# SSD mixer: gate factors of three groups from one 104-row tile, applied in the output projection, and the state's decay taken a chunk ahead

## Chip, cores and metric

One core of one Trainium2 chip runs the whole kernel in one launch. The metric is device time in microseconds (us), the median of several runs. Beside the runs there is one profiled execution, from which all rows of the profile come. Engine names are those of the profile: PE is TensorE's matmul, PEld its weight load, DVE VectorE, ACT ScalarE, POOL GpSimd, SP the engine that issues most DMAs.

## What is computed

The reference is a decoder trunk on 1040 tokens (16 meta tokens and 1024 of the sequence) of width 1024: a Mamba-2 (SSD) mixer, a gated convolution FFN, then stick-breaking attention and a second FFN. The change concerns the mixer and the projection behind it. Cut to that:

```python
z, xbc, dt_raw = split(u @ w_in)                    # z: 2048 wide, xbc: x (2048), b, c
xbc = silu(causal_conv(xbc))
dt = softplus(dt_raw + dt_bias);  a_cs = cumsum(dt * a)      # per chunk and head
# per chunk: inside the chunk, and from the state that came into it
y_diag = einsum(cb, decay_in, xdt)
state_next = state * chunk_decay + chunk_state
y = y_diag + einsum(c, state, exp(a_cs)) + x * d_skip
hg = (y * silu(z)).reshape(b, L, G, 512)            # G = 4 groups
hg = hg * rsqrt(mean(hg * hg, axis=-1) + eps)
out = (hg * gate_g) @ w_out
```

The gate's normalisation needs, for each of 4 groups and each token, one factor r = rsqrt(mean of 512 squares + eps).

## The kernel before, in words

*Layout.* Features lie on the 128 partitions, tokens along the row. The inner width 2048 is 4 groups of 512, a group is 4 row tiles of 128 x 1040 (`rows[g][:4]`, called `xbc` in the profile), plus a B and a C tile. Tokens are cut in two ways: 3 token tiles of 348, 348 and 344 (`TT`) for projections and gates, 9 chunks of 116 (`CH`, the last 112) for the scan. A float32 product is made of three matmuls of split operands (hi x hi, lo x hi, hi x lo, L185 to L187), so a projection tile (8 row tiles of input) is 24 matmuls, and an output projection tile (4 row tiles) is 12.

*The mixer* (`mixer`, L683) interleaves two kinds of work by hand. The first is a stream of projection tiles: `blocks` is the list into(1), gate(0), into(2), gate(1), into(3), gate(2), gate(3). `into(g)` makes the convolved x, B and C of group g; `gate(g)` makes silu(z) for its four row tiles (L535), multiplies it into y (L542), squares (L547) and adds the squares up in a tile `z` (L551, L553). The second is the scan of the four groups, chunk by chunk: `ssd_front` transposes B and x, makes C x B (`cb`) on PE, masks it (`cbm`, DVE), scales x (`xdt`, DVE, then `xde`, POOL) and copies the transposed B (`bk`, ACT); `ssd_back` makes the chunk's state `S` (PE, L663), multiplies the old state by the chunk's decay (POOL, through `pieces`, L98), adds S (DVE, L670), makes the chunk's output `y` on PE (L675 from the chunk itself, L677 from the state) and adds it on DVE (L679). `ssd_decays` makes the two decay matrices `D` (DVE, ACT) and `E` (POOL) for the next chunk. Between front and back of a chunk, `SHARES` says how many tiles of the stream are taken.

*The order.* In this part the instructions of PE, DVE, ACT and POOL run in the order in which the code is written (`manual_schedule`); each engine works through its own queue and waits at an instruction whose operands aren't there. The SP queue (DMAs) is ordered by the scheduler. From `out_proj` on, the scheduler orders all.

*The gate's normalisation* is `gate_norm` (L559): `rstd` (L209 to L226) sums the squares over the partitions by a matmul with `ones` (`ms`, L218), which leaves the sum of each token on all 128 partitions, takes Ln and Exp on ACT (L221, L222) on 128 x 348, refines by four DVE operations of that size (L223 to L226), and multiplies each of the four row tiles by the factor and the gain in place (L564). It is one call for each token tile; for groups 0 to 2 the stream makes the calls ahead of tiles 0, 2 and 4 behind the gate's block, for group 3 ahead of tiles 1, 2 and 3. After the third call, groups 0 and 1 are written to DRAM by POOL (`spill`, L401, `y_d`), to be fetched again (L410) in the output projection.

*The output projection* (`out_proj`, L752) takes groups 0 to 2 one after the other: it fetches y, splits it into hi (`yh`, ACT, L195) and lo (`yl`, DVE, L196), and then for each of 8 output tiles and 3 token tiles makes 12 matmuls (`acc`) and adds the result to the stream `h` on DVE (L422). Group 3 goes into the next phase's matmuls.

Of the kernel before, what the change touches and what calls it, by code (L numbers as in the profile page):

```python
# [24 lines left out]
QW = 1056  # L25
# [44 lines left out]
ORD = ((0, 0), (1, 0), (0, 1), (1, 1), (0, 2), (1, 2))  # L70
XB, SQD = 9, (1, 4, 7)
SCALE = 0.125
SHARES = (3,) + 7 * (2,) + (1,), 3 * (4, 3, 3), 3 * (4, 3, 3), (3,) + 6 * (2,) + (3, 3)
PIECE = 256


# [24 lines left out]
class Trunk:  # L101
# [456 lines left out]

    def gate_norm(self, g, x, acc, j):  # L559
        s0, n = TT[j]  # L560
        r = self.rstd([acc.pop(j)], n, DI // GROUPS)
        for q in range(4):
            xq = x[q][:, s0 : s0 + n]
            self.nc.vector.scalar_tensor_tensor(xq, xq, self.par("gate_norm", 4 * g + q), r, op0=ALU.mult, op1=ALU.mult)  # L564

    def settle(self):

# [56 lines left out]
    def ssd_front(self, g, x, bt, ct, c, dk, pool):  # L624

        nc = self.nc
        h0 = GH * g
        tt = nc.vector.tensor_tensor
        t0, n = CH[c]
        cc = 3 * (c % 3) + c // 3  # L630
        e = t0 + n
        pcb = self.sm("cb")
        if c < 8:
            nc.tensor.transpose(pcb[:n, P : 2 * P], bt[:, t0:e], self.ident)
        nc.tensor.matmul(pcb[:n, :n], bt[:, t0:e], ct[:, t0:e], start=True, stop=True)
        px = self.lg("px")
        for q in range(4):
            nc.tensor.transpose(px[:n, q * P : q * P + P], x[q][:, t0:e], self.ident)
        px = px[:n].rearrange("p (h d) -> p h d", h=GH)
        cbm = pool.tile([P, CB], F32, tag="cbm", name=self.nm("cbm"), bufs=2)  # L640
        tt(cbm[:n, :n], pcb[:n, :n], self.past[:n, :n], op=ALU.mult)
        xdt = pool.tile([P, GH, 64], F32, tag="xdt", name=self.nm("xdt"), bufs=2)
        tt(xdt[:n], px, self.cols[:n, 0, cc, h0 : h0 + GH].unsqueeze(2).to_broadcast([n, GH, 64]), op=ALU.mult)
        tt(dk, dk, cbm[:n, :n].unsqueeze(1).to_broadcast([n, GH, n]), op=ALU.mult)
        bk = xde = None
        if c < 8:
            bk = pool.tile([P, P], F32, tag="bk", name=self.nm("bk"), bufs=2)
            nc.scalar.activation(bk[:n], pcb[:n, P : 2 * P], AF.Copy)
# [4 lines left out]
    def ssd_back(self, g, x, c, dk, ce, xdt, xde, bk, state, pool):  # L653

        nc = self.nc
        h0 = GH * g
        t0, n = CH[c]
        cc = 3 * (c % 3) + c // 3
        e = t0 + n
        new = None  # L660
        if c < 8:
            ps = self.lg("S")
            nc.tensor.matmul(ps, bk[:n], xde[:n].rearrange("p h d -> p (h d)"), start=True, stop=True)  # L663
            new = pool.tile([P, GH, 64], F32, tag="state", name=self.nm("state"), bufs=2)
            psv = ps.rearrange("p (h d) -> p h d", h=GH)
            if c == 0:
                nc.scalar.activation(new, psv, AF.Copy)
            else:
                pieces(nc.gpsimd, new, state, self.cd[:, cc, h0 : h0 + GH].unsqueeze(2).to_broadcast([P, GH, 64]), ALU.mult)
                nc.vector.tensor_tensor(new, new, psv, op=ALU.add)  # L670
        py = self.sm("y")
        for i in range(GH):
# [5 lines left out]
        for q in range(4):  # L678
            nc.vector.scalar_tensor_tensor(x[q][:, t0:e], x[q][:, t0:e], self.par("d_skip", 4 * g + q),  # L679
                                           py[:, q * CB : q * CB + n], op0=ALU.mult, op1=ALU.add)  # L680
        return new

    def mixer(self, mx):  # L683

# [4 lines left out]
        with self.tc.tile_pool(name="ssd", bufs=3) as pool:  # L689
            yd, rows = [None] * 4, [[] for _ in range(4)]  # L690
            accs = [{} for _ in range(4)]
            done, waiting = [], []

            def later(j, f):
                if 3 * j + 2 < len(done):
                    f()
                else:
                    waiting.append((j, f))

            def gate(g):  # L700
                def norm(j):
                    self.gate_norm(g, rows[g], accs[g], j)
                    if j == 2 and g < 2:
                        yd[g] = self.spill(rows[g][:4], f"y{g}_d")
                return self.gate_group(u, g, rows[g], accs[g], later if g == 3 else lambda j, f: f()) + [((0, 2, 4) if g < 3 else (1, 2, 3), norm)]

            into = lambda g: self.in_group(u, g, rows[g])
            blocks = into(1) + gate(0) + into(2) + gate(1) + into(3) + gate(2) + gate(3)
# [7 lines left out]
            with self.tc.manual_schedule(engines={E.PE, E.DVE, E.Activation, E.Pool}):  # L716
                ahead = self.ssd_decays(0, rows[0][5], 0, pool)
                dk, ce = next(ahead)
                for g in range(GROUPS):
                    *x, bt, ct = rows[g]  # L720
                    share, given = SHARES[g], 0
                    state = None
                    for c in range(9):
                        if g == c == 0:
                            next(work)
# [954 lines left out]
```

## Time and profile before

| | us |
|---|---|
| runs, median of 3 | 2958.23 (2957.75 to 2958.55) |
| the profiled execution | 2959.8 |
| its span on the core | 2958.1 |
| its mean granted clock | 0.990 |
| mixer region, by the trace | about 140 to 690 |
| output projection of groups 0 to 2 | about 690 to 832 |

The page gives for each engine its busy time, its share of the span and its number of instructions. A row of the timeline is: start, duration, engine, line, operation, out<-in with shapes, and in brackets how long the engine stood idle before it and what it waited for. A row of the waits is: engine, line and tile that waited, what was waited for, us in total, times, the longest. A row of the stretches is: from and to, length, busy time of each engine (with its instructions), the granted clock as a share of full speed, DMA share and GB/s.

### The profile page before, as it was taken

How to read it: one execution, taken by the hardware profiler on the slowest of the kernel's cores; microseconds unless marked ns; L12 is line 12 of the kernel's file. 1: busy time of each engine (PE TensorE's matmuls, PEld its weight loads, DVE VectorE, ACT ScalarE, POOL GpSimd, SP SyncE). 2: the span in 40 equal slices, each digit the busy share in tenths (PEclk: the TensorE clock that was granted, in tenths of full speed). 3: DMA queues.
4: the chain of work that ended last, by engine and by line, in shares of the span. 5: the costliest groups of instructions: out<-in, count | busy, mean ns of one | idle time of the engine just before them, and what ended most of it. 6: DMA issues, size and time to landing. Idle time of an engine off the chain costs nothing. (4 is left out here: it accounts for less than half of the span.)

```text
span 2958.1 us, 58618 instructions
## 1 busy us (share of the span) xinstructions
PE 2863.3 (97%) x21863; PEld 2724.6 (92%) x21863; DVE 2123.8 (72%) x4026; ACT 1650.7 (56%) x3398; POOL 1613.2 (55%) x2434
## 2 busy tenths in 40 slices
PE   7999998999998999999989999999999999999998
PEld 5998897889998999999989999999898999999888
DVE  5685857786468676767766888888849766767766
ACT  4555454553245665565334788888836655655433
POOL 1264545563246888876763222222353988886872
PEclk9999999999999999999999999999999999999999
DMA  5242332324122222224232122222341222225321
GB/s 164 76 113 81 107 90 96 99 85 142 56 88 76 79 75 78 80 87 174 93 125 87 55 61 67 63 65 58 101 151 59 86 82 79 76 83 178 107 100 65
DMA packets 123421, 272.80 MB, mean 92 GB/s; under 512 B 13664, under 2 KB 53216, under 8 KB 123136
## 3 DMA queue, kind: packets, MB, share of 16 engines
q1 hardware_dynamic: 117760, 257.93, 26.6%
q10 hardware_dynamic: 4112, 6.56, 0.7%
q0 software_dynamic: 1264, 4.57, 0.4%
q8 instruction: 172, 2.82, 0.4%
q14 instruction: 113, 0.93, 0.1%
HBM read 200.89 MB, written 53.20 MB: 86 GB/s over the span
## 5 line engine op out<-in xcount | busy, mean ns | idle before, releaser
L98 POOL TENSOR_TENSOR wl<-w,wh 128x256 fp32r<-128x256 f32 x780 | 692.3, 918 | 446.0 <-ACT wh L178 296.8
L185 PE MATMUL pj<-uh,wh 128*128 128x348 f32 (+2 forms) x1536 | 504.0, 329 | 9.5 <-DVE xbc L315 6.9
L186 PE MATMUL pj<-ul,wh 128*128 128x348 f32 (+2 forms) x1536 | 497.1, 324 | 0.0
L187 PE MATMUL pj<-uh,wl 128*128 128x348 f32 (+2 forms) x1536 | 494.1, 322 | 0.0
L185 PE MATMUL p<-bh,fh 128*128 128x262 f32 (+1 forms) x1408 | 400.2, 285 | 2.4 <-ACT fh L934 2.2
L187 PE MATMUL p<-bh,fl 128*128 128x262 f32 (+1 forms) x1408 | 400.6, 285 | 0.5 <-POOL fl L98 0.4
L186 PE MATMUL p<-bl,fh 128*128 128x262 f32 (+1 forms) x1408 | 400.0, 285 | 0.1
L98 POOL TENSOR_TENSOR fl<-x,fh 128x256 fp32r<-128x256 f32 x352 | 260.0, 771 | 159.0 <-ACT fh L934 134.6
L186 PE MATMUL p<-bl,wh 128*128 128x262 f32 (+1 forms) x1056 | 301.1, 285 | 6.3 <-DVE bl L887 6.1
L185 PE MATMUL p<-bh,wh 128*128 128x262 f32 (+1 forms) x1056 | 301.5, 286 | 5.1 <-ACT ft L982 4.2
L185 PEld LDWEIGHTS pj<-uh,wh 128*128 128x128 f32 x1536 | 290.6, 189 | 12.9 <-issue 10.1
L187 PE MATMUL p<-bh,wl 128*128 128x262 f32 (+1 forms) x1056 | 301.0, 285 | 0.0
L186 PEld LDWEIGHTS pj<-ul,wh 128*128 128x128 f32 x1536 | 291.1, 190 | 1.4 <-issue 0.5
L315 DVE SCALAR_TENSOR_TENSOR c<-p,params,c 128x260 f32<-128x260 f32 (+1 forms) x528 | 249.5, 480 | 58.4 <-ACT c L312 51.6
L187 PEld LDWEIGHTS pj<-uh,wl 128*128 128x128 f32 x1536 | 290.5, 189 | 0.6 <-issue 0.6
L185 PEld LDWEIGHTS p<-bh,fh 128*128 128x128 f32 x1408 | 267.7, 190 | 3.4 <-ACT fh L934 2.9
L186 PEld LDWEIGHTS p<-bl,fh 128*128 128x128 f32 x1408 | 267.6, 190 | 0.6 <-DVE bl L887 0.3
L187 PEld LDWEIGHTS p<-bh,fl 128*128 128x128 f32 x1408 | 266.8, 190 | 1.4 <-POOL fl L98 1.2
L982 ACT ACTIVATE ft<-p 128x262 f32<-128x262 f32 (+1 forms) x352 | 133.2, 383 | 184.2 <-DVE p L985 109.2
L187 PE MATMUL acc<-gh,wl 128*128 128x260 f32 (+1 forms) x672 | 213.8, 320 | 2.8 <-POOL wl L98 2.8
L185 PE MATMUL acc<-gh,wh 128*128 128x260 f32 (+1 forms) x672 | 211.1, 320 | 3.1 <-DVE h L1133 3.1
L186 PE MATMUL acc<-gl,wh 128*128 128x260 f32 (+1 forms) x672 | 213.9, 319 | 0.0
(314 smaller groups left out, 7965.9 us busy)
## 6 DMA issues: line engine op xcount, KB each, us to landing
w<-in_w_up SPq DMA_DIRECT2D x88, 512.0 KB
w<-in_w_down SPq DMA_DIRECT2D x44, 512.0 KB
w<-in_w_in SPq DMA_DIRECT2D x40, 512.0 KB
E<-ea_d SPq DMA_DIRECT2D x32, 464.0 KB
D<-acs_d SPq DMA_DIRECT2D x32, 420.5 KB
g<-c SPq DMA_DIRECT2D x88, 130.0 KB
g<-c SPq DMA_DIRECT2D x88, 128.0 KB
b<-g SPq DMA_DIRECT2D x16, 520.0 KB
```

Of the source, the lines that this page charges most:

```text
L98: eng.tensor_tensor(out[:, c], x[:, c], y[:, c], op=op)
L185: mm(out, wh, uh, start=first, stop=False, skip_group_check=joins)
L186: mm(out, wh, ul, start=False, stop=False, skip_group_check=joins)
L187: mm(out, wl, uh, start=False, stop=last, skip_group_check=joins)
L315: nc.vector.scalar_tensor_tensor(out, ps[:, o + i : o + i + n], wcol(i), out, op0=ALU.mult, op1=ALU.add)
L982: nc.scalar.activation(s[:, :N], ps[:, :N], AF.Copy)
```

## The change

Four edits:

1. *Gate factors.* For groups 0 to 2 `gate_norm` only makes the sums with the `ones` matmul, copies one row of them (ACT), and sends it to DRAM (`ms_d`, 3 x 1040). One more tile of the stream after the last chunk, `gate_factors` reads all 3 x 1040 sums as a tile of 104 partitions x 30 (40 bytes in a piece), makes the three groups' factors there in one go (Ln, Exp, three DVE operations) and writes them to DRAM (`gr_d`). In `out_proj` each group fetches its row of factors, spread over 128 partitions (`r`), and multiplies its four row tiles in place (12 DVE products, L792) before the split. Group 3 is normalised as before.
2. *When.* The calls for groups 0 to 2 come ahead of tiles 1, 2 and 3 behind the gate's block instead of 0, 2 and 4; the spill of groups 0 and 1 comes ahead of the first call, before the normalisation.
3. *State.* POOL multiplies the new state by the next chunk's decay at the end of `ssd_back` (`scaled`); the next `ssd_back` only adds S to it.
4. *Small moves.* `bk` is copied ahead of `cbm` in `ssd_front`; in the last chunks of group 3 one tile of the stream moves from between front and back of chunk 7 to behind the scan (SHARES).

The diff, without comment lines and the arguments that only follow:

```diff
-SHARES = (3,) + 7 * (2,) + (1,), 3 * (4, 3, 3), 3 * (4, 3, 3), (3,) + 6 * (2,) + (3, 3)
+SHARES = (3,) + 7 * (2,) + (1,), 3 * (4, 3, 3), 3 * (4, 3, 3), (3,) + 7 * (2,) + (3,)
...
     def gate_norm(self, g, x, acc, j):
         s0, n = TT[j]
+        if g < 3:
+            ps, sums = self.sm("ms"), acc.pop(j)
+            self.nc.tensor.matmul(ps[:, :n], self.ones, sums[:, :n], start=True, stop=True)
+            self.nc.scalar.activation(sums[:1, :n], ps[:1, :n], AF.Copy)
+            self.nc.sync.dma_start(self.ms_d[g : g + 1, s0 : s0 + n], sums[:1, :n])
+            return
...
+    def gate_factors(self):
+        nc = self.nc
+        m, k, width = 104, 10, DI // GROUPS
+        s, y, b = (self.tmp("gf")[:m, : 3 * k] for _ in range(3))
+        view = lambda d: d.rearrange("g (p c) -> p g c", c=k)
+        nc.sync.dma_start(s.rearrange("p (g c) -> p g c", c=k), view(self.ms_d))
+        self.ln_exp()
+        nc.scalar.activation(y, s, AF.Ln, scale=1.0 / width)
+        nc.scalar.activation(y, y, AF.Exp, scale=-0.5)
+        nc.vector.tensor_tensor(b, y, y, op=ALU.mult)
+        nc.vector.scalar_tensor_tensor(b, b, -0.5 / width, s, op0=ALU.mult, op1=ALU.mult)
+        nc.vector.scalar_tensor_tensor(y, b, 1.5, y, op0=ALU.add, op1=ALU.mult)
+        nc.sync.dma_start(view(self.gr_d), y.rearrange("p (g c) -> p g c", c=k))
...
+        bk = xde = None
+        if c < 8:
+            bk = pool.tile([P, P], F32, tag="bk", name=self.nm("bk"), bufs=2)
+            nc.scalar.activation(bk[:n], pcb[:n, P : 2 * P], AF.Copy)
         cbm = pool.tile([P, CB], F32, tag="cbm", name=self.nm("cbm"), bufs=2)
...
-        bk = xde = None
         if c < 8:
-            bk = pool.tile([P, P], F32, tag="bk", name=self.nm("bk"), bufs=2)
-            nc.scalar.activation(bk[:n], pcb[:n, P : 2 * P], AF.Copy)
...
             else:
-                pieces(nc.gpsimd, new, state, self.cd[:, cc, h0 : h0 + GH].unsqueeze(2).to_broadcast([P, GH, 64]), ALU.mult)
                 nc.vector.tensor_tensor(new, new, psv, op=ALU.add)
...
-        return new
+        scaled = None
+        if c < 7:
+            scaled = pool.tile([P, GH, 64], F32, tag="state", name=self.nm("state"), bufs=2)
+            cn = 3 * ((c + 1) % 3) + (c + 1) // 3
+            pieces(nc.gpsimd, scaled, new, self.cd[:, cn, h0 : h0 + GH].unsqueeze(2).to_broadcast([P, GH, 64]), ALU.mult)
+        return new, scaled
...
                 def norm(j):
+                    if j == 0 and g < 2:
+                        yd[g] = self.spill(rows[g][:4], f"y{g}_d")
                     self.gate_norm(g, rows[g], accs[g], j)
-                    if j == 2 and g < 2:
-                        yd[g] = self.spill(rows[g][:4], f"y{g}_d")
-                return self.gate_group(u, g, rows[g], accs[g], later if g == 3 else lambda j, f: f()) + [((0, 2, 4) if g < 3 else (1, 2, 3), norm)]
+                return self.gate_group(u, g, rows[g], accs[g], later if g == 3 else lambda j, f: f()) + [((1, 2, 3), norm)]
...
+                next(work)
+                self.gate_factors()
                 for _ in work:
                     pass
...
         for g in range(3):
-            ops = [self.split(ys[g][q] if yd[g] is None else self.fetch(yd[g][q], "y"), "y") for q in range(4)]
+            r = self.rp.tile([P, QW], F32, tag="r", name=self.nm("r"))
+            self.nc.sync.dma_start(r[:, :L], self.gr_d[g : g + 1].to_broadcast([P, L]))
+            y = [ys[g][q] if yd[g] is None else self.fetch(yd[g][q], "y") for q in range(4)]
+            for s0, n in TT:
+                for q in range(4):
+                    c = slice(s0, s0 + n)
+                    self.nc.vector.scalar_tensor_tensor(y[q][:, c], y[q][:, c], self.par("gate_norm", 4 * g + q), r[:, c], op0=ALU.mult, op1=ALU.mult)
+            ops = [self.split(t, "y") for t in y]
```

The number of rows per engine stays on PE and POOL, DVE has 33 fewer, ACT 15 fewer, SP 14 more.

**POOL's order**, in group 1 of the scan, where group 0's spill falls (a row is line, operation, out<-in, shape, pieces; `state`, `xde`, `E` are as above, `wl` is the low part of a projection weight). Before:

```order
L98 TENSOR_TENSOR state_3027<-state_2820,cd 128x256 x2
L98 TENSOR_TENSOR xde_3067<-xdt_3062,cols 116x256 x2
L98 TENSOR_TENSOR wl_3121<-w_386_3118,wh_3120 128x256 x4
L401 DMA y_d<-xbc_544 128x1040
L401 DMA y_d<-xbc_678 128x1040
L401 DMA y_d<-xbc_788 128x1040
L401 DMA y_d<-xbc_903 128x1040
L98 TENSOR_TENSOR E_3116<-E_3116,xbc_2158 128x232 x4
L98 TENSOR_TENSOR state_3222<-state_3027,cd 128x256 x2
L98 TENSOR_TENSOR xde_3262<-xdt_3257,cols 116x256 x2
```

Now:

```order
L98 TENSOR_TENSOR E_2900<-E_2900,xbc_2163 128x232 x4
L401 DMA y_d<-xbc_546 128x1040
L401 DMA y_d<-xbc_680 128x1040
L401 DMA y_d<-xbc_790 128x1040
L401 DMA y_d<-xbc_905 128x1040
L98 TENSOR_TENSOR state_3049<-state_2847,cd 128x256 x2
L98 TENSOR_TENSOR xde_3067<-xdt_3064,cols 116x256 x2
L98 TENSOR_TENSOR wl_3111<-w_385_3108,wh_3110 128x256 x4
L98 TENSOR_TENSOR E_3106<-E_3106,xbc_2163 128x232 x4
L98 TENSOR_TENSOR state_3219<-state_3049,cd 128x256 x2
```

The four spill DMAs stand a chunk earlier and no longer behind the products of L564; the state row, which had stood between its own chunk's `E` and the next `xde`, now makes the state for the chunk that follows.

**DVE's order** at the normalisation of a token tile of group 2. Before:

```order
L644 TENSOR_TENSOR D_6065<-D_6065,cbm_6147 116x928
L553 TENSOR_TENSOR z_5562<-z_5562,z_6094 128x348
L542 TENSOR_TENSOR xbc_3470<-xbc_3470,z_6182 128x344
L223 TENSOR_TENSOR z_5529<-y_6203 128x348
L224 TENSOR_TENSOR z_5529<-z_5529,ms_6201 128x348
L225 TENSOR_SCALAR z_5529<-z_5529 128x348
L226 TENSOR_TENSOR y_6203<-y_6203,z_5529 128x348
L564 TENSOR_SCALAR xbc_2959<-xbc_2959,params,y_6203 128x348
L564 TENSOR_SCALAR xbc_3127<-xbc_3127,params,y_6203 128x348
L564 TENSOR_SCALAR xbc_3308<-xbc_3308,params,y_6203 128x348
L564 TENSOR_SCALAR xbc_3470<-xbc_3470,params,y_6203 128x348
L553 TENSOR_TENSOR z_5600<-z_5600,z_6182 128x344
```

Now the eight rows L223 to L564 are gone there, and twelve products with the factors (L792) stand at the junction to the output projection, ahead of the twelve lo parts. The last four of these and what stands behind them:

```order
L196 TENSOR_TENSOR yl_6813<-y_6792,yh_6812 128x344
L196 TENSOR_TENSOR yl_6821<-y_6794,yh_6820 128x344
L196 TENSOR_TENSOR yl_6829<-y_6796,yh_6828 128x344
L196 TENSOR_TENSOR yl_6837<-y_6798,yh_6836 128x344
L553 TENSOR_TENSOR z_6299<-z_6299,z_6732 128x344
L223 TENSOR_TENSOR z_6170<-y_6742 128x348
L422 TENSOR_TENSOR h_6851<-h_6851,acc_6854 128x348
L422 TENSOR_TENSOR h_6955<-h_6955,acc_6958 128x348
L422 TENSOR_TENSOR h_6851<-h_6851,acc_6868 128x348
L224 TENSOR_TENSOR z_6170<-z_6170,ms_6740 128x348
```

Group 3's own normalisation, which stays, now follows group 0's products and lo parts, and all of these stand ahead of the first add L422.

**SP's order** at the junction, now:

```order
L410 DMA y_6796<-y_d 128x1040
L410 DMA y_6798<-y_d 128x1040
L172 DMA w_838_6948<-in_w_out_f 128x512
L172 DMA w_845_7000<-in_w_out_f 128x512
L578 DMA gf_6636<-ms_d 104x3x10
L172 DMA w_852_7052<-in_w_out_f 128x512
L585 DMA gr_d<-gf_6637 104x3x10
L787 DMA r_6790<-gr_d 128x1040
L172 DMA w_859_7104<-in_w_out_f 128x512
L410 DMA h_6851<-h_d 128x1040
L410 DMA h_6903<-h_d 128x1040
```

The read of the sums, the write of the factors and the broadcast read stand in one queue, with the fetches of `h` behind them; before, those followed the fetches of y and the weights at once.

More of the change, by code (lines that the diff above doesn't have):

```diff
@@ L651, in ssd_front, with ssd_back @@
         return xdt, xde, bk
-    def ssd_back(self, g, x, c, dk, ce, xdt, xde, bk, state, pool):
+    def ssd_back(self, g, x, c, dk, ce, xdt, xde, bk, states, pool):
         nc = self.nc
@@ L659, in ssd_back @@
         e = t0 + n
-        new = None
+        state, new = states
         if c < 8:
@@ L663, in ssd_back @@
             nc.tensor.matmul(ps, bk[:n], xde[:n].rearrange("p h d -> p (h d)"), start=True, stop=True)
-            new = pool.tile([P, GH, 64], F32, tag="state", name=self.nm("state"), bufs=2)
             psv = ps.rearrange("p (h d) -> p h d", h=GH)
             if c == 0:
+                new = pool.tile([P, GH, 64], F32, tag="state", name=self.nm("state"), bufs=2)
                 nc.scalar.activation(new, psv, AF.Copy)
             else:
-                pieces(nc.gpsimd, new, state, self.cd[:, cc, h0 : h0 + GH].unsqueeze(2).to_broadcast([P, GH, 64]), ALU.mult)
                 nc.vector.tensor_tensor(new, new, psv, op=ALU.add)
@@ L692, in mixer @@
             done, waiting = [], []
+            self.ms_d, self.gr_d = (self.dp.tile([3, L], F32, tag=t, name=t) for t in ("ms_d", "gr_d"))
             def later(j, f):
@@ L721, in mixer @@
                     share, given = SHARES[g], 0
-                    state = None
+                    state = None, None
                     for c in range(9):
```

## Prediction

> **What bounds the kernel now.** I read the head of the page first, then the busy time stretch by stretch, then TensorE's (PE's) waits, and last the timeline around the longest of them.
>
> The head of the page, span and PE's row:
>
> ```profile
> span 2958.1 us, 58618 instructions
> PE 2863.3 (97%) x21863; PEld 2724.6 (92%) x21863; DVE 2123.8 (72%) x4026; ACT 1650.7 (56%) x3398; POOL 1613.2 (55%) x2434
> ```
>
> PE is the bound over the whole span: 2958.1 - 2863.3 = 94.8 us are all that it stands idle. The change adds no matmul and takes none away (the three `ones` products of a group stay), so it can gain only idle time of PE and time in which PE runs below its full clock. Both are to be looked for in the mixer, the only part it touches besides the first groups of the output projection.
>
> Busy time by stretch; the columns are the stretch and its length, then PE, PEld, DVE, ACT and POOL busy with their instructions, the granted clock, DMA share and GB/s:
>
> ```profile
> 281.00:349.00 68.00, 58.21 (x378) 53.40 (x377) 50.07 (x107) 31.97 (x45) 32.68 (x45) 0.90 0.32 105
> 349.00:440.00 91.00, 91.00 (x680) 86.08 (x680) 60.19 (x135) 46.45 (x69) 43.60 (x57) 1.00 0.28 82
> 440.00:503.00 63.00, 52.29 (x356) 47.84 (x355) 45.31 (x94) 30.07 (x44) 32.66 (x45) 0.95 0.31 101
> 503.00:545.00 42.00, 42.00 (x301) 39.96 (x301) 35.96 (x72) 21.50 (x31) 22.88 (x33) 1.00 0.35 103
> 545.00:640.00 95.00, 86.67 (x661) 78.84 (x660) 74.42 (x150) 50.34 (x73) 55.31 (x70) 0.99 0.31 99
> 640.00:690.00 50.00, 49.74 (x353) 46.31 (x354) 35.66 (x80) 29.17 (x48) 23.52 (x30) 0.95 0.20 64
> ```
>
> The first, third and fifth stretch hold the gate normalisations of groups 0, 1 and 2. There PE is idle 9.8, 10.7 and 8.3 us, and its clock falls. The second and fourth run the same chunks and the same tiles without a gate normalisation: PE 100% busy at clock 1.00. So the normalisations, not the scan as such, make the gaps. The size of it, by matmul count: the two undisturbed stretches pass 981 matmuls in 133 us, 135.6 ns each; the other four hold 1748, which at that pace take 237 us and took 276. **39 us** are recoverable if all were as smooth. The second way to count: idle 9.8 + 10.7 + 8.3 + 0.3 = 29.1 us, and clock 68 x 0.10 + 63 x 0.05 + 95 x 0.01 + 50 x 0.05 = 13.4 us, together 42.5.
>
> What PE waits for in the mixer (us in total, times, longest):
>
> ```profile
> PE ms L218 <- DVE z L553: 9.6, 2, 4.9
> PE S L663 <- POOL xde L98: 8.9, 6, 4.3
> PE pj L185 <- DVE xbc L315: 6.9, 2, 3.9
> PE S L663 <- ACT xbc L312: 2.1, 1, 2.1
> PE cb L635 <- ACT xbc L503: 1.6, 1, 1.6
> PE y L675 <- DVE D L644: 1.3, 1, 1.3
> ```
>
> The first four rows make 27.5 us. The timeline at the first `ms` gap shows what stands behind it:
>
> ```profile
> 282.91 1.18 POOL L98 TENSOR_TENSOR state<-state,cd 128x256 f32<-128x256 f32 x2
> 284.13 0.69 DVE L670 TENSOR_TENSOR state<-state,S 128x512 f32<-128x512 f32 x1 [3.01 <-POOL state L98]
> 285.72 0.27 DVE L641 TENSOR_TENSOR cbm<-cb,past 116x116 f32<-116x116 f32 x1
> 286.02 0.28 ACT L648 ACTIVATE bk<-cb 116x128 f32<-116x128 f32 x1 [6.96 <-DVE cbm L641]
> 287.54 0.93 DVE L553 TENSOR_TENSOR z<-z,z 128x348 f32<-128x348 f32 x1
> 288.52 1.53 PE L218 MATMUL ms<-z,ones 128*128 128x348 f32 x2 [4.86 <-DVE z L553]
> ```
>
> VectorE (DVE) stands 3.0 us for POOL's multiplication of the state; so the next chunk's `cbm` is late; so ScalarE (ACT) stands 6.96 us in front of `bk`, with the gate's silu and square behind it; so the sum of squares is late, and PE stands 4.86 us at `ms`. Waits of the whole mixer that belong to this chain, and the one on the spill:
>
> ```profile
> ACT bk L648 <- DVE cbm L641: 76.8, 29, 8.5
> DVE state L670 <- POOL state L98: 18.8, 6, 3.6
> POOL y_d L401 <- DVE xbc L564: 18.4, 2, 9.2
> ```
>
> **The change, part by part.**
>
> *State times decay a chunk ahead.* The same 56 POOL pieces, but issued at the end of a chunk for the next. DVE's 18.8 us of waiting go. POOL now stands there for the chunk's `y` matmuls to free the old buffer, with `xde` and `E` of the next chunk queued behind; in the undisturbed stretches POOL is busy 43.6 of 91 us, which hides that. Without that cover it would be a later `xde`, which is in the 8.9 us above already. Worth nothing alone where PE is at 100%; in the gate stretches it is the first link of the chain.
>
> *bk ahead of cbm on ACT.* ACT no longer waits for DVE (29 times, 2.6 us on average); instead `cbm` on DVE now waits for ACT's `bk`, a copy of 0.28 us. What is queued behind `cbm` on DVE is `xdt` and the D product, which feed POOL's `xde` and PE's `y`. Since ACT was the one that stood waiting in 29 of 32 chunks, it should mostly be there first. I price the new wait at 0; the other end is in the rivals.
>
> *Normalisation out of the mixer.* Per group DVE loses twelve row operations of four kinds and twelve L564 products. The two outer ones of the four kinds, and L564:
>
> ```profile
> L564 DVE SCALAR_TENSOR_TENSOR xbc<-xbc,params,y 128x348 f32<-128x348 f32 (+1 forms) x48 | 32.0, 728 | 0.4
> L223 DVE TENSOR_TENSOR z<-y 128x348 f32<-128x348 f32 (+1 forms) x12 | 8.1, 675 | 22.9 <-ACT y L222 21.2 <-PE S L663 1.7
> L224 DVE TENSOR_TENSOR z<-z,ms 128x348 f32<-128x348 f32 (+1 forms) x12 | 6.2, 513 | 0.3
> ```
>
> That is 12 x 0.73 + 12 x 0.59 = 16 us per group off the engine at which the waits of these stretches end, and the idle time ahead of L223 with it. The POOL spill of `y_d` no longer waits for the twelve products: its 18.4 us stood in front of `E`, state and `xde`, so the 8.9 us of PE at `S` should go as well. `ms` comes one tile (3.75 us, below) later, which gives the late sum of squares that much more room than the 4.9 us it lacked; with DVE's 3 us that is more than enough.
>
> What stays are the two short waits of the scan's own, 1.6 and 1.3 us. Nine one-row ACT copies and nine small SP writes take the place of 18 Ln and Exp passes on an ACT that is about half busy, and the tile that SHARES moves behind the last chunk of group 3 is the same tile: both priced at 0. I take **-38** of the 39 to 42.5; the low bound is the gaps that go by the chain alone, 9.6 + 8.9 + 2.1 + 3.4 of the third row = **-24**, the high one **-43**.
>
> *The new piece at the junction.* This runs before the output projection and has no cover but the last three projection tiles. Prices, from these rows:
>
> ```profile
> 775.00:800.00 25.00, 25.00 (x160) 25.00 (x159) 11.26 (x20) 4.64 (x8) 5.77 (x8) 1.00 0.13 42
> 686.00:745.00 59.00, 56.84 (x347) 54.42 (x347) 38.60 (x77) 23.39 (x47) 17.03 (x26) 1.00 0.44 159
> 691.49 1.28 ACT L209 ACT_TABLE_LOAD   x1
> L490 SPq DMA_DIRECT2D acs_d<-rows x3: 341/420/422, 100.1 to 100.9; - x3
> L606 SPq DMA_DIRECT2D D<-acs_d x36: 266/270/1507, 102.9 to 628.0; - x36
> 683.22 1.11 SPq L410 DMA_DIRECT2D y<-y_d  x2
> 686.87 1.26 ACT L195 ACTIVATE yh<-y 128x348 fp32r<-128x348 f32 x3 [3.28 <-DMA y<-y_d]
> 645.23 2.06 DVE L564 SCALAR_TENSOR_TENSOR xbc<-xbc,params,y 128x348 f32<-128x348 f32 x4
> 704.71 3.02 DVE L564 SCALAR_TENSOR_TENSOR xbc<-xbc,params,y 128x348 f32<-128x348 f32 x4
> 690.81 1.37 DVE L196 TENSOR_TENSOR yl<-y,yh 128x348 fp32r<-128x348 f32 x3
> L422 DVE TENSOR_TENSOR h<-h,acc 128x348 f32<-128x348 f32 (+1 forms) x35 | 17.4, 512 | 23.6 <-PE acc L187 20.6 <-DMA h<-h_d 3.0
> ```
>
> PE passes 160 matmuls in 25 us, 156 ns each: 3.75 us for a projection tile of 24, 1.88 us for an output tile of 12. A write to DRAM and the dependent read take 2.0 us from issue to issue (100.9 to 102.9); a broadcast read about 3.65 us (683.22 to 686.87). A product on DVE takes 0.515 us when POOL is quiet (645.23, four in 2.06), 0.755 when it is not (704.71).
>
> Let T be the end of the projection tile behind which `gate_factors` stands in the order; three tiles are left, so PE would begin the output projection at T + 11.4. The chain for `r`: ACT's queue ahead (a silu, squares, one `wh`), a table load and Ln, Exp on 30 columns, T + 4; three small DVE operations, T + 5; write to DRAM, T + 7; broadcast back, T + 10.7. Then twelve products of group 0 on DVE, 6.2 to 9.1 us, T + 17 to 18; then `yl` at 0.46 each. PE can take the first `yl` at about T + 18.5 and stands **7 us**. The twelve `yl` and the squares between them end at T + 26. Behind them stand, in DVE's written order, twelve products each of groups 3, 1 and 2, twelve small operations of group 3 and 14 adds L422 that empty PE's accumulators: 36 x 0.515 + 12 x 0.59 + 14 x 0.51 = 32.7 us, and about 1.5 more where POOL is in the way (busy 17 of 59 us there): T + 60. PE may be two or three accumulators ahead of the adds, 17 tiles, 32 us, which it would have had at T + 43.4 without any wait. So **DVE, not PE, sets the time for some 50 us here**, and PE loses 17 us. At the start of group 1 its `yl` stand behind ten adds: 2 more. Before, this stretch lost time too: 347 matmuls at 0.156 are 54 us of 59, and some matmul records may be missing; I take 4. Net **+15**. The bounds: +4, if the fetch comes early and POOL stays away from DVE (the first wait of 7 less some 3), and +28, if the products all cost 0.755 (36 x 0.24 = 8.6) and the r chain is 4 us longer. Off this stretch nothing changes.
>
> **Sum.** -38 + 15 = -23 us. The profiled execution took 2959.8 us, 1.7 above its span and 1.6 above the median of the runs (2958.23). 2958.2 - 23 gives **2935 us**. A measurement of this kernel can tell about 0.2%, 6 us, from no change.
>
> **A rule beside the rows.** On the clock: in the stretch from 281 us PE is idle 9.8 of 68 us, and the mean granted clock is 0.90. The Trainium skill ("TensorE: Matmul & The Clock Gate", section "What's actually happening") says the clock is halved after an idle window of about 3.4 us and comes back after about as long a busy one; by that, only the four gaps above 3.4 us (two at `ms`, one at `S`, one at `pj`) cost clock, some 1.7 us each, an estimate of 7 us in place of the 13.4, so the second way to count would give 36. The trace agrees in direction: no clock below 1.00 where there is no gap.
>
> **Rivals.**
>
> - *The junction is nearly free* (+4): -34, **2924 us**. For it: the DVE row of the 686 us stretch shows 20 us of slack in 59. Against: the change puts 24 products more into just this place.
> - *The next wait takes over*: half of the mixer's gaps stay, since DVE remains 66 to 75% busy and PE waits for `xbc` L315 (6.9 us), which has no link to any edit. -20 + 15 = -5, **2953 us**.
> - *POOL and DVE get in each other's way at the junction*: 86 DVE rows (twelve products and twelve `yl` of group 0, then the 62) at 0.24 us more each, +20: -38 + 15 + 20 = -3, **2955 us**. For it: 3.02 against 2.06 us for the same four products. Against: POOL is busy only 17 of 59 us there. The Trainium skill ("SBUF — State Buffer", section "Who interferes with whom") states the same as a rule: a DVE instruction with two inputs in SBUF contends with a POOL instruction that reads SBUF, and the shared ports are locked for a whole instruction. The products at L792 have two such inputs; the two rows above agree.
> - *Slower: cbm now waits for ACT.* Where ACT reaches `bk` late, behind a table load of 1.28 us, every one of the 32 chunks puts that on DVE, and through `xdt` and `xde` on PE: 32 x 1.28 = 41 us. -38 + 41 + 15 = +18, **2976 us**. It decides from the point at which ACT comes to `bk` later than DVE to `cbm`; before, ACT was there first 29 times, by up to 8.5 us.
> - *It doesn't do what it says*: the state's wait returns as one for `S` or `y`, DVE is as late as before, and only the later `ms` (9.6) and some of the spill's 8.9 are gained: -15 + 15 = 0, **2958 us**.
>
> **Chances.** Forecast 0.46 (own range 2926 to 2947), free junction 0.12, next wait 0.15, contention 0.12, cbm 0.10, no effect 0.05. Faster by over 0.2% (below 2952): 0.46 + 0.12 + 0.12 from the lower parts of the third and fourth = 0.70. Within: 0.07 + 0.07 + 0.03 = 0.17. Slower: 0.13. The range 2921 to 2958 leaves out the cbm case, the ends of the others, and half of no effect: 0.2.
>
> **What would show it.** In the stretches of groups 0 to 2, PE's waits at `ms` and at `S` for `xde` gone and the clock at 1.00; no wait of DVE for state and none of ACT at `bk`. At the junction, PE waiting for `yl` about 7 us once, then for adds L422, DVE close to 100% for some 40 us, `r` landing 10 to 11 us behind the tile. It would be wrong if DVE shows a wait at `cbm` for ACT of over 0.5 us in most chunks, if L315 becomes PE's longest wait, or if products L792 cost over 0.7 us on average.

## The result, and the profile after

| | us |
|---|---|
| before, median of the runs beside it | 2958.39 |
| the changed kernel, median of 4 runs | 2932.39 (2932.11 to 2939.06) |
| ratio to before, 95% interval | 0.9909 (0.9897 to 0.9922) |
| forecast | 2935, range 2921 to 2958 |

The kernel is 26 us faster, clear of the 0.2% that can be told apart. The head of the changed kernel's page:

```profile
span 2930.6 us, 58544 instructions
PE 2852.6 (97%) x21863; PEld 2717.9 (93%) x21863; DVE 2074.8 (71%) x3993; ACT 1629.3 (56%) x3379; POOL 1620.1 (55%) x2434
```

The span is 27.5 us shorter; PE's idle time went from 94.8 to 78.0 us, and its busy time fell by 10.7 us with the same 21863 matmuls. That fits the clock: the mean granted clock went from 0.990 to 0.993, which over the two spans makes 9 us less lost to the clock. The stretches of the mixer that had the gaps, and the two between, now (columns as before the change):

```profile
281.00:349.00 68.00, 68.00 (x498) 63.75 (x497) 47.86 (x110) 34.78 (x52) 39.14 (x56) 1.00 0.39 119
349.00:440.00 91.00, 91.00 (x659) 86.53 (x658) 54.09 (x129) 44.53 (x68) 47.72 (x61) 1.00 0.29 87
440.00:503.00 63.00, 63.00 (x468) 59.22 (x467) 42.94 (x95) 31.05 (x47) 38.65 (x56) 1.00 0.43 134
503.00:545.00 42.00, 42.00 (x312) 39.29 (x310) 25.47 (x64) 21.61 (x33) 18.07 (x23) 1.00 0.31 105
545.00:640.00 95.00, 94.59 (x747) 87.39 (x747) 60.17 (x151) 50.31 (x76) 58.79 (x76) 1.00 0.32 96
```

PE is busy all the time and the clock is 1.00 in every row. In the first row 498 matmuls pass where 378 passed before. The four longest waits of PE from 140 to 690 us:

```profile
PE acc L186 <- DVE yl L196: 3.3, 1, 3.3
PE acc L185 <- DVE h L422: 2.4, 1, 2.4
PE y L696 <- DVE D L669: 1.5, 1, 1.5
PE S L685 <- POOL xde L98: 1.4, 2, 1.0
```

The waits at `ms` (9.6) and `pj` (6.9) are gone, the one at `S` for `xde` went from 8.9 to 1.4; the two longest rows are new and belong to the junction. The other engines, from 140 to 640 us:

```profile
POOL state L98 <- DVE state L691: 56.7, 15, 5.5
...
ACT bk L664 <- PE cb L656: 5.3, 5, 1.8
...
DVE cbm L666 <- ACT bk L664: 1.9, 2, 1.2
```

DVE's wait for POOL's state (18.8) has turned round: POOL waits for DVE, 56.7 us, and no engine waits for POOL's state any more (PE still waits 1.4 us for its `xde`). ACT's 76.8 us at `bk` behind `cbm` are gone: what is left are 5.3 us for PE's `cb`, and `cbm` waits for ACT twice.

**Where the time went, in two pieces.** The first matmul of the output projection, and the last one of its 24th tile, before:

```profile
686.30 0.32 PE L185 MATMUL acc<-yh,wh 128*128 128x348 f32 x1
...
735.53 0.32 PE L187 MATMUL acc<-yh,wl 128*128 128x344 f32 x1
```

and now, with the chain of the factors between (SPq is SP's queue):

```profile
635.97 1.28 ACT L209 ACT_TABLE_LOAD   x1
637.26 0.23 ACT L580 ACTIVATE gf<-gf 104x30 f32<-104x30 f32 x1
638.24 0.19 DVE L584 SCALAR_TENSOR_TENSOR gf<-gf,gf 104x30 f32<-104x30 f32 x1
638.46 0.34 SPq L585 DMA_DIRECT2D gr_d<-gf  x1
640.41 0.33 SPq L787 DMA_DIRECT2D r<-gr_d  x1
644.00 6.93 DVE L792 SCALAR_TENSOR_TENSOR y<-y,params,r 128x348 f32<-128x348 f32 x12 [0.70 <-DMA r<-gr_d]
...
645.34 0.59 PE L185 MATMUL acc<-yh,wh 128*128 128x348 f32 x1
...
650.85 0.94 DVE L196 TENSOR_TENSOR yl<-y,yh 128x348 fp32r<-128x348 f32 x2
652.58 4.37 DVE L196 TENSOR_TENSOR yl<-y,yh 128x348 fp32r<-128x348 f32 x10
...
705.62 0.32 PE L187 MATMUL acc<-yh,wl 128*128 128x344 f32 x1
```

PE reaches the output projection 686.30 - 645.34 = **41 us earlier**. Its first 24 tiles then take 705.6 - 645.3 = 60.3 us where they took 49.2: **11 us are given back**. The output tiles of groups 1 and 2, counted in the same way by the starts of their matmuls, take 0.9 and 0.2 us longer than before, and what follows them 1.4, which makes the 27.5 of the spans.

### The profile page after: what moved, and what is told of

Its sections match the earlier page's. It is cut to its first block, busy times and chain, and to the rows that moved or that the text cites. A ratio compares the mean times of both kernels' runs of the same rounds, so it can differ in the third digit from the quotient of the medians.

```text
span 2930.6 us, 58544 instructions
## 1 busy us (share of the span) xinstructions
PE 2852.6 (97%) x21863; PEld 2717.9 (93%) x21863; DVE 2074.8 (71%) x3993; ACT 1629.3 (56%) x3379; POOL 1620.1 (55%) x2434
## 4 chain that ended last, share of the span: by engine, by line
PE 44%; DVE 2%; ACT 2%; POOL 1%; issue 1%; DMA 0%; DVEq 0%; ACTq 0%; SPq 0%; POOLq 0%
PE p L187 5%; PE p L186 5%; PE p L185 5%; PE acc L185 4%; PE acc L187 4%; PE acc L186 4%; PE pj L185 3%; PE pj L187 3%; PE pj L186 3%; PE po L1444 3%; PE wT L1430 2%; PE lg L1403 2%; POOL wl L98 1%; PE ms L897 0%; DVE h L1138 0%
## 5 line engine op out<-in xcount | busy, mean ns | idle before, releaser
L315 DVE SCALAR_TENSOR_TENSOR c<-p,params,c 128x260 f32<-128x260 f32 (+1 forms) x528 | 249.2, 480 | 58.7 <-ACT c L312 51.9
```

The source lines that it names most:

```text
L315: nc.vector.scalar_tensor_tensor(out, ps[:, o + i : o + i + n], wcol(i), out, op0=ALU.mult, op1=ALU.add)
```

## The experiments

Each kernel is compared with the kernel before on the same chip; ratios carry 95% intervals. The last two columns come from the one profiled execution of each: the start of the first matmul of the output projection, and the time from there to the start of the 288th, which ends its 24th tile.

| kernel | median us | ratio to before | first output matmul | 24 tiles |
|---|---|---|---|---|
| before | 2958.39 | 1 | 686.3 | 49.2 |
| changed | 2932.39 | 0.9909 (0.9897 to 0.9922) | 645.3 | 60.3 |
| scan edits alone | 2943.08 | 0.9942 (0.9930 to 0.9955) | 665.7 | 49.3 |
| gate edits alone | 2948.36 | 0.9963 (0.9949 to 0.9977) | 661.5 | 62.2 |
| changed, state in its own chunk | 2939.18 | 0.9930 (0.9917 to 0.9942) | 648.2 | 60.4 |
| changed, bk behind cbm | 2935.89 | 0.9920 (0.9906 to 0.9933) | 645.8 | 61.5 |
| changed, spill after the calls | 2934.35 | 0.9913 (0.9898 to 0.9927) | 644.5 | 65.1 |
| changed, calls at 0, 2, 4 | 2934.75 | 0.9914 (0.9899 to 0.9929) | 644.9 | 62.1 |
| changed, old SHARES | 2937.11 | 0.9927 (0.9913 to 0.9941) | 648.5 | 61.6 |
| changed, factors early | 2922.68 | 0.9871 (0.9855 to 0.9888) | 645.0 | 52.7 |
| changed, 24 products left out | 2925.58 | 0.9883 (0.9869 to 0.9898) | 645.2 | 53.9 |
| changed, 24 products held back | 2927.82 | 0.9896 (0.9882 to 0.9909) | 645.1 | 58.5 |
| factors early, 24 products held back | 2919.71 | 0.9868 (0.9855 to 0.9882) | 645.4 | 53.1 |
| factors early, 24 products left out | 2916.56 | 0.9860 (0.9847 to 0.9874) | 644.8 | 49.1 |

Behind the output tiles of groups 0 to 2 stands code that none of these edits touches. In the fourteen profiled executions it takes 2127 to 2134 us, so a few us between two medians can come from there; the last two columns don't have that part.

### Which edits carry the mixer

**The scan's edits alone**: the kernel before with `ssd_front` and `ssd_back` of the changed one.

```diff
+            bk = pool.tile(...)                        # ahead of cbm
...
-                pieces(nc.gpsimd, new, state, self.cd[:, cc, ...], ALU.mult)
...
+            pieces(nc.gpsimd, scaled, new, self.cd[:, cn, ...], ALU.mult)
```

> The kernel before, with the two edits of the scan alone: the state multiplied a chunk ahead, and bk copied ahead of cbm. The gate normalisation, its call points and the spill stay as before. Theory (the normalisations in the mixer make the gaps, the state's wait is only their first link): the wait at ms (9.6 us of PE) goes, most of the waits behind the spill stay; about -12, 2946 us, and the clock in the three gate stretches still below 1.00. Rival (the state's wait is the cause): nearly the whole mixer gain without the price of the junction, -38, 2920 us.

Measured: -16 us (2943.08), between the two, nearer to the theory. Two stretches with a gate normalisation, and PE's longest wait:

```profile
281.00:349.00 68.00, 63.22 (x428) 59.42 (x428) 56.52 (x115) 36.00 (x51) 38.48 (x52) 0.95 0.35 107
...
440.00:503.00 63.00, 58.14 (x400) 54.53 (x399) 52.57 (x108) 34.37 (x48) 32.80 (x46) 0.95 0.33 103
```

```profile
PE pj L185 <- DVE xbc L315: 9.6, 4, 4.5
PE S L664 <- POOL xde L98: 4.5, 4, 2.7
```

The wait at `ms` is gone and the clock stays below 1.00 in the gate stretches, as the theory had it; of the 8.9 us at `S`, half went too. What stays is DVE: busy 56.5 of 68 us, it makes PE wait for the conv tile L315.

**The gate's edits alone**: the changed kernel, with the two edits of the scan undone.

```diff
-            nc.scalar.activation(bk[:n], pcb[:n, P : 2 * P], AF.Copy)     # ahead of cbm
+            nc.scalar.activation(bk[:n], pcb[:n, P : 2 * P], AF.Copy)     # behind the D product
...
-            pieces(nc.gpsimd, scaled, new, self.cd[:, cn, ...], ALU.mult)
+                pieces(nc.gpsimd, new, state, self.cd[:, cc, ...], ALU.mult)
```

> The changed kernel with the state multiplied in its own chunk and bk copied behind cbm, as before: only the gate factors, the call points and the spill are changed. Theory: 10 us above the changed kernel, 2942 us, since with 16 us of DVE work per group gone the state's wait has nothing behind it that is late. Rival (the state's wait is the cause): the mixer gains nothing and the junction costs 12 us, 2970 us.

Measured: 16 us above the changed kernel where 10 were expected. PE still waits at `ms`, and the timeline shows another chain than before:

```profile
PE ms L563 <- DVE xbc L700: 9.6, 3, 4.1
```

```profile
299.82 2.18 POOL L401 DMA_DIRECT2D y_d<-xbc  x4
302.01 1.19 POOL L98 TENSOR_TENSOR state<-state,cd 128x256 f32<-128x256 f32 x2
303.24 0.69 DVE L691 TENSOR_TENSOR state<-state,S 128x512 f32<-128x512 f32 x1 [3.78 <-POOL state L98]
303.84 1.07 DVE L700 SCALAR_TENSOR_TENSOR xbc<-xbc,params,y 128x116 f32<-128x116 f32 x4
304.82 0.27 DVE L663 TENSOR_TENSOR cbm<-cb,past 116x116 f32<-116x116 f32 x1
...
305.06 1.49 PE L563 MATMUL ms<-z,ones 128*128 128x344 f32 x2 [4.06 <-DVE xbc L700]
305.13 0.28 ACT L669 ACTIVATE bk<-cb 116x128 f32<-116x128 f32 x1 [6.87 <-DVE cbm L663]
305.30 0.43 ACT L564 ACTIVATE z<-ms 1x348 f32<-1x348 f32 x1
```

The spill's four issues (2.18 us of POOL) stand ahead of the state; DVE waits 3.78 us for it; its adds of `y` (L700) are late, and PE's `ms` waits for them although it uses nothing of `y`. By the code, `ms`, `cb` and `y` share three small accumulators. No view shows which of them a matmul got; from the wait I take it that this `ms` was given the one that L700 empties. ACT, which would empty the earlier `ms` (L564), stands 6.87 us at `bk`. So the gate's edits by themselves put a new wait in the place of the old one.

**One of the two edits of the scan undone at a time:**

> The changed kernel with the state multiplied in its own chunk again; bk stays ahead of cbm. Theory: DVE waits for POOL's state again, some 20 us in all, PE hardly; +4, 2936 us. Rival (the state's wait is the cause): +25 or more, 2957 us.

> The changed kernel with bk copied behind cbm again. Theory: ACT stands at bk for DVE again, half as long as before since DVE is less late; +3, 2935 us. Rival (ACT standing at bk is what made the square sums late): +10 or more, 2942 us. If cbm's new wait for ACT costs something, this kernel is faster than the changed one.

Measured: +6 us by the ratios (0.9930 against 0.9909) and +3, both with intervals that overlap the changed kernel's. Together the two were worth 16. The traces show it more sharply: without one of them PE reaches the output projection 2.9 us later (the state) or 0.5 (`bk`), without both 16.2 us later. So either of them covers most of the other's loss. In the kernel with the state in its own chunk, DVE still waits 19.6 us for it, but ACT doesn't stand behind it. At the same place as above:

```profile
298.42 0.26 ACT L664 ACTIVATE bk<-cb 116x128 f32<-116x128 f32 x1
298.58 0.43 ACT L564 ACTIVATE z<-ms 1x348 f32<-1x348 f32 x1
...
301.08 0.74 PE L563 MATMUL ms<-z,ones 128*128 128x344 f32 x2
...
303.49 0.69 DVE L692 TENSOR_TENSOR state<-state,S 128x512 f32<-128x512 f32 x1 [3.79 <-POOL state L98]
```

`bk` and the row copy come 6.7 us earlier, and `ms` runs before DVE has the state, so here it can't have been given the accumulator of `y`; one that ACT had emptied was free. With `bk` behind `cbm` and the state ahead, ACT waits 48.8 us at `bk`, but DVE has no wait to pass on. `cbm` waiting for ACT costs nothing: the kernel without it isn't faster.

By the first matmul of the output projection (661.5 with the gate's edits, 665.7 with the scan's, 645.3 with both) the mixer gains 25, 21 and 41 us: nearly the sum. Neither half alone is "the cause"; both make DVE less late.

**Spill and call points:**

```diff
-                    if j == 0 and g < 2:
-                        yd[g] = self.spill(rows[g][:4], f"y{g}_d")
                     self.gate_norm(g, rows[g], accs[g], j)
+                    if j == 2 and g < 2:
+                        yd[g] = self.spill(rows[g][:4], f"y{g}_d")
```

> The changed kernel with the spill of groups 0 and 1 after the third gate call again, not ahead of the first. Theory: what held the spill before was the wait for the twelve products on DVE, which are gone; nothing stands in front of it, 0, 2932 us. Rival (POOL's place for the spill itself matters): +4 or more, 2936 us.

```diff
-((1, 2, 3), norm)
+((0, 2, 4) if g < 3 else (1, 2, 3), norm)
```

> The changed kernel with the gate calls of groups 0 to 2 ahead of tiles 0, 2 and 4 again. Theory: the first ms comes a tile earlier and the square sums are no longer late by 4.9 us but still by about a tile's work of ACT and DVE: PE waits about 2 us for each of three groups, +5, 2937 us. Rival (the later call is all that removed the wait at ms): +10 with the clock down again, 2942 us. Second rival (it doesn't matter any more): 0.

Measured: 2934.35 and 2934.75, both within the interval of the changed kernel, and both with PE busy 68.00 of 68.00 us at clock 1.00 in the first stretch; PE reaches the output projection within 1 us of the changed kernel. Neither the place of the spill nor the later call, undone alone, costs the mixer anything. Both undone together was not run, so it isn't shown that neither covers for the other. The +5 expected of the calls was a miss.

### What the junction costs

**Factors early**: `gate_factors` after chunk 7 of group 3, where its sums are already in DRAM.

```diff
+                            if c == 7:
+                                self.gate_factors()
...
-                next(work)
-                self.gate_factors()
```

> The changed kernel with gate_factors called after chunk 7 of group 3 instead of one tile after chunk 8, four projection tiles earlier: the factors and the first broadcast are in place and the twelve products of group 0 done before the last projection tile ends. Theory 1 (both the chain and the amount of DVE work at the junction cost): the wait for yl goes, and twelve products, 7 us, leave the stretch in which DVE is the bound; -8, 2924 us. Theory 2 (DVE's amount of work alone sets the junction): -7 from the twelve products that move, the same. Rival (the products now stand in the mixer and delay the scan's last chunk): 0 to +5, 2933 to 2937 us.

Measured: 2922.68, about 10 us below the changed kernel; the first 24 tiles take 7.6 us less. The broadcast is issued at 623.5, the products stand at 627 and 631, and PE:

```profile
640.00:690.00 50.00, 45.45 (x278) 43.98 (x277) 40.68 (x85) 17.54 (x33) 18.11 (x23) 1.00 0.49 172
```

against the same 50 us of the changed kernel:

```profile
640.00:690.00 50.00, 40.40 (x232) 38.09 (x230) 46.70 (x93) 17.27 (x31) 19.08 (x18) 0.93 0.51 187
```

46 matmuls more and no clock lost. The mixer pays nothing: PE reaches the output projection at 644.96.

**24 products left out, or held back on DVE:**

```diff
-            for s0, n in TT:
+            for s0, n in TT if g == 0 else ():
```

> The changed kernel without the 24 products of groups 1 and 2 in the output projection, so these two groups go into it without their normalisation. Theory (DVE is the bound at the junction): 12 or 13 us of DVE work gone from it, of which the part behind the first wait shows; -7, 2925 us. Rival (only the chain of the factors costs, the adds L422 are hidden anyway): -1 or less, 2932 us.

```diff
                 for s0, n in TT:
                     self.accumulate(h, f, s0, n, ..., ops, HB)
+                    if g < 2 and 2 <= f < 6:
+                        self.tc.keep_in_program_order(product(g + 1, r, y, f - 2, s0, n))
```

> The changed kernel with the products of groups 1 and 2 held back in the same way, and the factors where the change has them. Theory: the wait for the chain of the factors stays (7 us of PE at the first output tiles), the 24 products leave the crowded stretch: like the kernel that leaves them out, -6, 2926 us. Rival: the chain alone sets the junction, 0, 2932 us.

Measured: -7 us without them, -4 or -5 with them held back (the second with an interval that overlaps the changed kernel's); in the 24 tiles -6.4 and -1.8. Chain and amount are two costs: without the 24 products the wait for `yl` stays (3.3 us in the waits, as in the changed kernel), with the early factors the wait is gone and the adds stay late.

**Both together:**

> The kernel with gate_factors after chunk 7, and besides the products of groups 1 and 2 held back on DVE: those of a group stand one after each add of output tiles 2 to 5 of the group before. Theory (what is left of the junction's cost is DVE's amount of work): 24 output tiles, which took 52.7 us with the early factors and would take 47 without a wait, come down by 4; 2919 us. Rival (the rest is something else, a weight's low part or the order of group 3's own products): 0, 2923 us. Second rival (a product between two adds delays the adds): +3, 2926 us.

> The kernel with gate_factors after chunk 7, without the 24 products of groups 1 and 2, so these two groups go into the projection without their normalisation: what holding them back can bring at most. Theory: -5 against the early factors alone, 2918 us, and PE waits for no add in the first 24 output tiles. Rival (chain and amount are one cost, counted twice): no gain over the early factors, 2923 us.

Measured: 2919.71 and 2916.56. Holding back on top of the early factors brings 1 us by the ratios (0.9868 against 0.9871) and 3 by the medians: not told apart from nothing. The 2919 us of the theory came by luck: the 24 tiles, which were to come down by 4 us, take 53.1 where they took 52.7; the twelve products of group 1 still stand among them, and why moving the other twelve brings nothing there was not traced. The tiles of group 1 take 1.6 us less, and the rest of the 3 us lies behind them. Leaving the products out brings 3 to 6 us by the runs and 3.6 in the 24 tiles, which then take 49.1, as before the change. So chain and amount together are all that the change lost there. What is left on DVE there are its other rows: group 3's own normalisation, and the adds. The 50 us from 640 in the kernel without the 24 products:

```profile
640.00:690.00 50.00, 48.55 (x301) 47.65 (x300) 30.25 (x62) 18.17 (x34) 16.39 (x25) 1.00 0.48 173
```

DVE falls to 30 of 50 us, and PE is back at 48.55. The kernel with early factors beats both the kernel before and the changed one; holding the products back as well is the fastest that computes all, by less than the measurement can tell.

**The old SHARES:**

> The changed kernel with the old SHARES of group 3: its eighth-from-last tile order is as before, so one tile of the stream stands between front and back of the last chunk but one and gate_factors comes a tile later in the order. Theory: the factors come one tile, 3.75 us, nearer to the output projection and the first wait grows by as much; +3, 2935 us. Rival: 0, 2932 us, since the wait for the amount of DVE work behind covers it.

Measured: 2937.11, about 5 us above the changed kernel by the ratios, the two intervals just overlapping. PE's waits at the junction have a row that the changed kernel has at 0.7 us:

```profile
PE acc L185 <- DVE h L422: 5.1, 2, 3.1
PE acc L185 <- ACT yh L195: 3.1, 1, 3.1
PE acc L186 <- DVE yl L196: 2.5, 1, 2.5
```

With one tile fewer behind it, the chain of the factors comes out later for PE: the first output matmul starts 3.2 us later, and the 24 tiles take 1.3 us more.

## Why the prediction was right, and where it was not

- **What is recoverable in the mixer: right, slightly small.** Forecast -38 out of 39 by matmul count and 42.5 by idle time and clock; measured 41, between the two counts. The term was undersized by 3. The rival of a next wait that takes over (2953) fell: the one at L315 went with the others.
- **Which step carries it: right in direction, the shares not worked out.** The prediction gave one sum for all edits of the mixer: the state's wait as the first link, and 16 us of DVE work per group as the weight behind it. The expectation for the gate's edits alone, 10 us above the changed kernel, held that without this work nothing late stands behind the state's wait. That was too strong: 16 us are lost, by a wait that the prediction did not see, `ms` standing until DVE's adds of `y` are done. The scan's edits alone gave 16 where 12 were expected. Inside the gate's edits, the products, the four small DVE operations and ACT's Ln and Exp went together; which of them counts most was not tested.
- **The new wait of cbm for ACT, priced at 0: right.** It is 1.9 us on DVE in two chunks; the slower rival (1.28 us in each of 32 chunks) did not come about. ACT, which used to stand waiting here, is now there first in nearly all chunks, as the prediction had it.
- **The spill and the later call:** the wait of the spill went, and `S` with it, but by the products' going, not by the new place; the later `ms` was credited with room that wasn't needed.
- **The junction: right in its mechanism; +15 was forecast, 12 measured** (11 in the first 24 tiles, 1 in the tiles of groups 1 and 2; the free junction, +4, did not come about). By its own steps, with T = 633.9, the end of the projection tile ahead of `gate_factors`: factors ready T + 4.5 (T + 5 was forecast), broadcast landed T + 10 (10.7), products done T + 17 (17 to 18), PE 7 us late (the first twelve output matmuls run from 645.34 to 654.39, 9 us where 2 are needed; 7 was forecast as standing), DVE through at T + 57 (T + 60). That the 7 came out is in part luck: PE stands 4.6 us (3.3 of them at `yl`), and part of the rest is a granted clock of 0.50 from 648.2 to 655.1, which the prediction did not count here. The row that bears out "DVE, not PE, sets the time":

```profile
644.00:691.00 47.00, 36.95 (x209) 34.65 (x208) 45.86 (x91) 16.43 (x29) 19.27 (x19) 0.93 0.51 187
```

  DVE is busy 45.9 of 47 us. The kernels with early factors and without the 24 products split it: by the runs some 10 us for the chain and group 0's products, some 7 for the other 24, 14 to 16 for both; in the 24 tiles 7.6, 6.4 and 11.2.
- **Contention, the rival at 2955: did not come about.** The products at L792 cost 0.58 each for group 0 (6.93 for twelve) and 0.50 where twelve stand together at 684 us, near the price with a quiet POOL.

```profile
L792 DVE SCALAR_TENSOR_TENSOR y<-y,params,r x24: 562/570/1054, 644.0 to 678.5; 128x348 f32<-128x348 f32 x16, 128x344 f32<-128x344 f32 x8
```

  Two of group 0's products take 1.05 and 1.04 us (from 646.47 and 647.45), the other ten 0.56 to 0.58. Only these two run beside POOL's products `wl` (646.26 to 648.11). So a product can still be held up; the trace agrees with the rule of the Trainium skill ("SBUF — State Buffer", section "Who interferes with whom") as far as that, but POOL made few such products there. The rest of POOL's time there is mostly standing: eight copies of 128 x 2 zeros, of which the shortest takes 0.18 us,

```profile
L412 POOL COPY h<-zero x8: 183/546/7425, 648.1 to 657.9; 128x2 f32<-128x2 f32 x8
```

  and the longest 7.4, from 650.43 to 657.85, while DVE works without a pause, on its lo parts above all; it ends when DVE first stands idle (657.8 to 658.05). So it looks as if here DVE held POOL up, which costs nothing: PE waits for POOL nowhere in this stretch.
- **SHARES, priced at 0: wrong.** "The same tile" is not the same when a chain's place in the order is counted from the end of the stream: the tile stands between the factors and their use, and is worth 4.5 us by the traces and about 5 by the runs.

The gap that I had put at the start of group 1 (2 us) is seen as 1.66 us of PE at 712, waiting for an add; the tiles of group 1 take 0.9 us longer than before. Open are the 1.4 us behind groups 1 and 2; executions differ by more than that there, so they need not belong to the change.

## What to carry to other kernels

Where PE is busy for 97% of a span, count matmuls per us in stretches with and without the suspected work: the difference is what taking it away can bring, clock included. Work that is moved off a stretch lands in another: price the chain to its first use and the amount of work on the receiving engine apart, since they cost apart, and start the chain as soon as its inputs are there (here four tiles earlier, at no price to the mixer, worth some 10 us).

## What the runs showed of the hardware that was not expected

Short gaps cost clock too. Before the change PE stood 3.04 us from 327.08 and 1.88 us from 335.78; the stretches behind these:

```profile
331.47:334.88 3.41, 3.41 (x14) 3.41 (x13) 1.81 (x7) 0.00 (x0) 1.57 (x3) 0.50 0.65 260
338.29:341.70 3.41, 3.41 (x29) 2.62 (x29) 3.34 (x7) 1.77 (x2) 3.41 (x7) 0.50 0.10 32
```

The granted clock is 0.50 in both, for 3.41 us each. Other gaps, of 1.1 to 2.1 us, were followed by no such stretch, so the length of a gap alone doesn't decide it. Where the gap lies does. In the mixer the clock fell six times, at 287.09, 331.47, 338.29, 450.93, 491.89 and 638.67: these starts lie whole multiples of 3.413 us apart, on one grid (from the first to the last, 351.58 us, 103 of them). The cells of the grid just ahead of the two stretches above, and the one with most of the 2.1 us gap from 497.85 in it:

```profile
328.06:331.47 3.41, 1.34 (x8) 1.37 (x9) 1.85 (x4) 0.00 (x0) 3.39 (x7) 1.00 0.92 365
334.88:338.29 3.41, 1.53 (x8) 0.91 (x6) 3.34 (x7) 2.67 (x5) 2.68 (x4) 1.00 0.00 0
498.72:502.13 3.41, 2.18 (x24) 1.42 (x26) 3.27 (x7) 2.72 (x4) 3.41 (x6) 1.00 0.00 0
```

In the first two PE is idle for 2.07 and 1.88 of 3.41 us, and the clock is 0.50 in the next cell; in the third for 1.23, and it stays at 1.00. From 140 to 690 us every full-clock cell in which PE was idle for 1.88 us or more was followed by half clock, and none with 1.56 or less. The boundary is not sharper than that: at 901.49 a cell with 1.51 us of idle was followed by half clock. The six stretches last 27.3 us and cost 13.7 us of clock, close to the 13.4 of the prediction's second count. (Its remark that no clock falls below 1.00 where there is no gap misses one row: 0.95 from 640 us with 0.3 us idle. That is the end of the stretch begun at 638.67, behind a gap from 635.98.)

The prediction set beside its own count a lower one after the Trainium skill ("TensorE: Matmul & The Clock Gate", section "What's actually happening"), by which only gaps of a whole window of 3.4 us would cost clock (36 us recoverable in place of 42.5). The length of the stretches agrees with that page; that only a whole window of idle time counts does not hold here, and the 41 us that came back bear out the higher count.
